# Moving the operands' rows from 128 to 64 bytes past the weights' rows, modulo 256

## The chip, the cores and the metric

The kernel runs on one core of a Trainium2 chip. The metric is the device time of one execution in microseconds; the time before is the median of three runs.

## What is computed

One layer of a hybrid decoder trunk in float32, over 16 meta tokens and 256 sequence tokens with a model width of 2048:

```
h = concat(meta, x)                                       # 272 rows of 2048
proj = rmsnorm(h) @ w_in                                  # one input projection, 13336 columns
o_fox = forgetting_attention(fq, fk, fv, ff)              # 8 heads of 128
o_gla = head_rmsnorm(gated_linear_attention(...)) * silu(gr)   # 4 heads
y = sigmoid(gate_fox) * (o_fox @ w_o_fox) + sigmoid(gate_gla) * (o_gla @ w_o_gla)
h = h + y @ w_out
h = h + square(relu(rmsnorm(h) @ w_ff1)) @ w_ff2          # 2048 -> 8192 -> 2048
out = rmsnorm(h)[16:]
```

## The kernel before

**Two halves for each number.** Each float32 matrix product is made from float32r products. An operand and a weight are each split into a high and a low half (a rounding copy on ScalarE, a subtraction on VectorE), and three of the four products are summed in PSUM. Activations stand in SBUF feature by feature on the partitions; a row of an operand holds, for one block k of 128 features, the 256 tokens' high halves and behind them the 256 low halves, 512 numbers or 2048 bytes.

**The pair.** For each k, `mac2` issues two matmuls: `whi` (128x128 weights) against the 512 numbers of the row (line 143), then `wlo` against the 256 high halves (line 144). `gemm2` runs 16 such pairs into one PSUM bank, 8 pairs for the forgetting attention's output. The operands read in this way are `x` (first norm), `og` and `of` (the two branches), `y` (the mixer's sum), `x2` (second norm) and `a` (the squared relu, anew in each of four groups). Each operand has its 16 or 8 rows in one tile made by `operand`, whose argument `at` leaves so many float32 numbers free ahead of the first row.

**The triple.** Where the meta tokens are wanted too, `gemm_all` runs `mac3`: three matmuls of 272 columns for each k, on `x` alone (lines 148, 150 and 152). Here line 148 reads the low halves, whose first number is 64 bytes further on in the row, modulo 256, than the first number that lines 150 and 152 read. A row of `x` is 576 numbers apart from the next, 2304 bytes, so all its rows stand alike modulo 256.

**The order of the reading.** `steps` rearranges the columns of the moving operand and of its result: four numbers (16 bytes) are read, then 48 bytes are skipped; four passes go over the row in this way, each 16 bytes further on.

```
return ap.rearrange("p (i a e) -> p a i e", a=4, e=4)
```

**The weights** come in as 1 MB chunks in the order that `stream()` lists, in two halves, by DMA on SyncE's queue into `raw`. ScalarE copies each into `whi` (line 120) and VectorE subtracts into `wlo` (line 121). Both are pools of five buffers of 4096 bytes, so all weights start at one place modulo 256; in the built program that is byte 128. The operands' tokens start at byte 0 (modulo 256) in the kernel before, so 128 bytes past the weights.

**Elsewhere.** At the start, seven output tiles are fed at once while the first rows arrive: lines 359 and 361 issue up to four matmuls of 512 columns in a row, and then up to four of 256 columns. At the end, line 921 issues 16 matmuls of 256 columns in a row in the stepped order with `wlo`, for each of four output tiles, and line 937 then reads two straight runs of 128 numbers with weights held in `whi_last`, whose place is chosen by itself.

Of the kernel before, what the change touches and what calls it, by code (L numbers as in the profile page):

```python
# [8 lines left out]
F32R = mybir.dt.float32r  # L9
# [7 lines left out]
P = 128  # L17
D = 2048
KT = D // P
# [4 lines left out]
FOX_H, FOX_D = 8, 128  # L24
# [8 lines left out]
NL = 4  # L33
# [32 lines left out]
def trunk(ctx: ExitStack, tc: tile.TileContext, hT, w_small, w_all, consts, w_alpha2, out):  # L66
# [3 lines left out]
    def nm(s):  # L70
        serial[0] += 1
        return f"{s}_{serial[0]}"

    const = ctx.enter_context(tc.tile_pool(name="const", bufs=1))
    keep = ctx.enter_context(tc.tile_pool(name="keep", bufs=1))
# [49 lines left out]
    def next_weights(keep_hi=None):  # L125
        c = chunk[0]
        chunk[0] += 1
        parts = []
        for i in range(2):
            hi, lo, step = weight_half(c, i, None if keep_hi is None else keep_hi[:, HK * i : HK * (i + 1), :])  # L130
            step(0, HK)
            parts.append((hi, lo))
        return lambda k: (parts[k // HK][0][:, k % HK, :], parts[k // HK][1][:, k % HK, :])
# [20 lines left out]
    def gemm2(w, x, k0=0, nk=KT, pool=None):  # L154

        ps = bank(pool or pg, "ps")
        for k in range(nk):
            hi, lo = w(k0 + k)
            mac2(ps, hi, lo, x[:, k], k == 0, k == nk - 1)
        issued()  # L160
        return ps
# [69 lines left out]
    def operand(pool, name, nk=KT, at=0, **kw):  # L231

        t = pool.tile([P, at + nk * 2 * NT], F32R, name=nm(name), **kw)
        return t[:, at:].rearrange("p (k o t) -> p k o t", o=2, t=NT)
# [2 lines left out]
    h = keep.tile([P, KT, NA + 3], F32, name="h")  # L237

    ROW = 576
    x_row = keep.tile([P, 32 + KT * ROW + 32], F32R, tag="s1", name="x")[:, 32 : 32 + KT * ROW].rearrange(  # L240
        "p (k r) -> p k r", r=ROW)[:, :, 0 : 2 * NA]
    x_hi, x_lo = x_row[:, :, 0:NA], x_row[:, :, NA:]
    x = x_row[:, :, NM : NM + 2 * NT].rearrange("p k (o t) -> p k o t", t=NT)
# [22 lines left out]
    def gain(i, k):  # L266
        return h[:, k, NA + i : NA + i + 1]
# [60 lines left out]
    for s in range(KT // 2):  # L328
# [22 lines left out]
        at = [(w[0][:, c], w[1][:, c]) for w, n in ((wa, 4), (wb, 3)) for c in range(n)]  # L351
# [113 lines left out]
    og_box = []  # L465

    def og_tile():
        if not og_box:
            og_box.append(operand(keep, "og", at=48, tag="s2"))
        return og_box[0]  # L470

    def gla_gates(ts):
# [30 lines left out]
    def gla_head(hd, sg, ready=None):  # L503
# [129 lines left out]
        def scale():  # L633
            for i in range(4):
                j = 4 * hd + i
                nc.vector.scalar_tensor_tensor(oT[:, i, :], oT[:, i, :], ggn[:, j : j + 1], rg, op0=ALU.mult,
                                               op1=ALU.mult)
                nc.vector.tensor_tensor(oT[:, i, :], oT[:, i, :], st["sg"][:, i, :], op=ALU.mult)
                split_to(og_tile()[:, j, 0, :], og_tile()[:, j, 1, :], oT[:, i, :])
# [44 lines left out]
    for hd in range(1, GLA_H):  # L684
        gla_head(hd, None)
    flush()
    og = og_tile()


    cum.close()  # L690
    branches = ExitStack()
    late = branches.enter_context(tc.tile_pool(name="late", bufs=1, reuse_waits="tile"))
    of = operand(late, "of", FOX_H, at=16)
    negc = late.tile([P, FOX_H, NA], F32, name="negc")
    nc.gpsimd.dma_start(negc.rearrange("p h t -> p (h t)"), fdram.to_broadcast([P, FOX_H * NA]))
    fox = ExitStack()
# [137 lines left out]
    for j0 in range(0, KT, 2):  # L834
# [5 lines left out]
        for j in range(2):  # L840
            t = total(gemm2(next_weights(), og))
            nc.vector.tensor_tensor(t, gates[2 * j + 1], t, op=ALU.mult)
            nc.vector.tensor_tensor(yf[:, j0 + j, :], gates[2 * j], t, op=ALU.add)
    y = operand(keep, "y", at=48, tag="s1")
    for j in range(KT):
        split_to(y[:, j, 0, :], y[:, j, 1, :], yf[:, j, :])
    mix.close()
# [3 lines left out]


    ht = h[:, :, NM:NA]
    x2 = operand(keep, "x2", at=48, tag="s2")

    def square_sum(j, acc):
        if j == 0:
            nc.scalar.activation(acc, ht[:, j, :], AF.Square)
        else:
            sq = gat.tile([P, NT], F32, tag="hsq", name=nm("hsq"))  # L860
            nc.scalar.activation(sq, ht[:, j, :], AF.Square)  # L861
            nc.gpsimd.tensor_tensor(acc, acc, sq, op=ALU.add)  # L862

    def add_residual(j, ps):
        b = tmp.tile([P, NT], F32, tag="evb", name=nm("evb"))
        nc.scalar.copy(b, ps[:, NT:512])
        nc.vector.tensor_tensor(ht[:, j, :], ps[:, 0:NT], ht[:, j, :], op=ALU.add)
        nc.vector.tensor_tensor(ht[:, j, :], ht[:, j, :], b, op=ALU.add)
# [16 lines left out]
    def relu2(a, f, ps):  # L885
        t = total(ps)
        nc.vector.scalar_tensor_tensor(t, t, 0.0, r2b, op0=ALU.max, op1=ALU.mult)
        s = gat.tile([P, NT], F32, tag="asq", name=nm("asq"))
        nc.vector.tensor_tensor(s, t, t, op=ALU.mult)
        split_to(a[:, f, 0, :], a[:, f, 1, :], s)  # L890

    acc = gat.tile([P, NT], F32, tag="acc", name="acc3", bufs=1)
    for g in range(NG):
        a = operand(keep, "a", at=48, tag="s1")
        held = []
        for f in range(KT):
            ps = gemm2(next_weights(), x2, pool=px if g == 0 and f < 3 else pg)
            if g == 0 and f == 0:
                held.append(ps)
                continue  # L900
            if g == 0 and f == 1:
                relu2(a, 0, held.pop())
            relu2(a, f, ps)
        last = g == NG - 1
        for j in range(KT - NL if last else KT):
            add_residual(j, gemm2(next_weights(), a))
            if last:
                square_sum(j, acc)
                nc.scalar.activation(ht[:, j, :], ht[:, j, :], AF.Identity, scale=gain(2, j))
                if j == 0:  # L910
                    tc.keep_in_program_order(nc.scalar.preload_act_table_set("natural_log_exp_and_others"))


    whi = keep.tile([P, 0 + NL * KT * P + 64], F32R, tag="s2", name="whi_last")[:, 0 : 0 + NL * KT * P].rearrange(
        "p (n k m) -> p n k m", k=KT, m=P)
    ends = []
    for n in range(NL):
# [150 lines left out]
```

## Time and profile before

| what | value |
|---|---|
| median of three runs (lowest to highest) | 1540.71 us (1538.93 to 1549.66) |
| the profiled execution: its time, its span | 1539.45 us, 1537.7 us |
| mean granted TensorE clock | 0.999 |
| TensorE matmuls: busy, number | 99% of the span, 9812 |
| TensorE weight loads: busy, number | 91%, 9812 |
| VectorE, ScalarE, GpSimd busy | 69%, 51%, 8% |
| share of TensorE in the chain that ended last | 93% |

Matmuls are pipelined: one starts long before the one ahead of it has ended. The duration of a matmul's record therefore says little of its cost. What one costs is the time from its start to the start of the next, and that is read from the view in order of time, or from the number of matmuls in a stretch of known length.

### The profile page before, as it was taken

The page shows a single profiled execution, that of the slowest core. Times are in us where ns is not written, and L with a number is a line of the kernel's source. Part 1 is how long each engine was busy: PE and PEld are TensorE (multiplying, and loading weights), DVE is VectorE, ACT ScalarE, POOL GpSimd, SP SyncE. Part 2 cuts the span into 40 slices and gives each one's busy share as a digit, 9 for nine tenths or more (in the row PEclk, how much of TensorE's full clock was granted, in tenths as well). Part 3 has the DMA queues.
Part 4 walks back from the last instruction along what each step waited for, and adds up shares of the span by engine and source line. Part 5 has one row for each costly group of instructions (what it writes and reads, how often), then busy time and mean ns, then how long its engine had stood idle before and what let it go on. Part 6 is the DMA issues. An engine that isn't in the chain of part 4 may idle for free.

```text
span 1537.7 us, 25427 instructions
## 1 busy us (share of the span) xinstructions
PE 1525.8 (99%) x9812; PEld 1399.2 (91%) x9812; DVE 1059.2 (69%) x1659; ACT 791.0 (51%) x1271; POOL 128.3 (8%) x213
## 2 busy tenths in 40 slices
PE   9999999999999999999999999999999999999997
PEld 8999999999998888899888899889899889888887
DVE  7898858686666655656777876567765776667765
ACT  7766444455555444444565554444544544445563
POOL 5012000011100000000011000000000000000022
PEclk9999999999999999999999999999999999999999
DMA  9544545455555555555565555555565556655552
GB/s 309 180 162 168 179 160 187 161 207 171 166 170 180 199 198 196 201 194 200 183 210 200 191 194 200 196 198 199 192 204 195 199 198 194 200 196 200 193 195 97
DMA packets 86602, 293.09 MB, mean 191 GB/s; under 512 B 9112, under 2 KB 16800, under 8 KB 86352
## 3 DMA queue, kind: packets, MB, share of 16 engines
q1 hardware_dynamic: 85872, 289.62, 55.8%
q8 instruction: 77, 1.26, 0.3%
q0 software_dynamic: 176, 1.12, 0.2%
q10 hardware_dynamic: 432, 0.72, 0.1%
q14 instruction: 45, 0.37, 0.1%
HBM read 289.32 MB, written 2.11 MB: 190 GB/s over the span
## 4 chain that ended last, share of the span: by engine, by line
PE 93%; DVE 2%; DMA 1%; ACT 1%; issue 1%; POOL 1%; SPq 0%; POOLq 0%; ACTq 0%; DVEq 0%
PE ps L143 51%; PE ps L144 26%; PE psa L152 4%; PE psa L148 4%; PE psa L150 4%; DMA raw<-w_all_dram 1%; DVE wlo L121 1%; PE ps L937 1%; PE pa L557 1%; PE ps L921 0%; ACT whi L120 0%; PE po L620 0%; POOL o L985 0%; ACT whi L292 0%; POOL room L340 0%
## 5 line engine op out<-in xcount | busy, mean ns | idle before, releaser
L121 DVE TENSOR_TENSOR wlo<-raw,whi 128x1024 fp32r<-128x1024 f32 x522 | 640.3, 1227 | 399.2 <-ACT whi L120 390.9
L120 ACT CAST whi<-raw 128x1024 fp32r<-128x1024 f32 x522 | 548.9, 1052 | 601.6 <-PE ps L143 532.4
L143 PE MATMUL ps<-x,whi 128*128 128x512 f32 x1952 | 655.7, 383 | 0.8 <-DVE x L874 0.8
L144 PE MATMUL ps<-x,wlo 128*128 128x256 f32 x1952 | 533.3, 273 | 0.0
L143 PEld LDWEIGHTS ps<-x,whi 128*128 128x128 f32 x1952 | 366.4, 188 | 65.5 <-DVE x L874 1.1
L144 PEld LDWEIGHTS ps<-x,wlo 128*128 128x128 f32 x1952 | 366.8, 188 | 0.1
L143 PE MATMUL ps<-a,whi 128*128 128x512 f32 x960 | 319.9, 382 | 0.0
L144 PE MATMUL ps<-a,wlo 128*128 128x256 f32 x960 | 261.4, 273 | 0.0
L143 PEld LDWEIGHTS ps<-a,whi 128*128 128x128 f32 x960 | 179.9, 188 | 31.8
L148 PE MATMUL psa<-x,whi 128*128 128x272 f32 x640 | 183.1, 287 | 0.0
L152 PE MATMUL psa<-x,whi 128*128 128x272 f32 x640 | 181.5, 284 | 0.0
L144 PEld LDWEIGHTS ps<-a,wlo 128*128 128x128 f32 x960 | 180.4, 188 | 0.3
L150 PE MATMUL psa<-x,wlo 128*128 128x272 f32 x624 | 176.8, 283 | 0.0
L148 PEld LDWEIGHTS psa<-x,whi 128*128 128x128 f32 x640 | 120.0, 187 | 0.3
L152 PEld LDWEIGHTS psa<-x,whi 128*128 128x128 f32 x640 | 120.0, 188 | 0.0
L150 PEld LDWEIGHTS psa<-x,wlo 128*128 128x128 f32 x624 | 117.2, 188 | 0.0
L862 POOL TENSOR_TENSOR acc<-acc,hsq 128x256 f32<-128x256 f32 x26 | 28.5, 1094 | 735.5 <-ACT hsq L861 735.5
L143 PE MATMUL ps<-og,whi 128*128 128x512 f32 x256 | 85.9, 382 | 0.0
L143 PE MATMUL ps<-y,whi 128*128 128x512 f32 x256 | 85.3, 382 | 0.0
L144 PE MATMUL ps<-og,wlo 128*128 128x256 f32 x256 | 69.9, 273 | 0.0
L144 PE MATMUL ps<-y,wlo 128*128 128x256 f32 x256 | 69.7, 273 | 0.0
L184 DVE TENSOR_TENSOR evt<-ps,evb 128x256 f32<-128x256 f32 x158 | 65.7, 416 | 0.5 <-ACT evb L181 0.5
(297 smaller groups left out, 1419.6 us busy)
## 6 DMA issues: line engine op xcount, KB each, us to landing
raw<-w_all_dram SPq DMA_DIRECT2D x537, 512.0 KB, 3.6
raw<-w_all_dram SPq DMA_DIRECT2D x8, 384.0 KB, 7.0
h<-hT_dram SPq DMA_DIRECT2D x8, 275.0 KB, 6.7
negc<-fdram POOLq DMA_DIRECT2D x1, 1088.0 KB, 8.2
out_dram<-o SPq DMA_DIRECT2D x2, 512.0 KB, 2.6
raw<-w_all_dram SPq DMA_DIRECT2D x2, 256.0 KB, 4.0
room<-w_small_dram SPq DMA_DIRECT2D x1, 320.0 KB, 7.6
out_dram<-o ACTq DMA_DIRECT2D x1, 320.0 KB, 3.1
```

Source lines behind the costliest of these rows:

```text
L120: nc.scalar.copy(hi[:, k, :], r)
L121: nc.vector.tensor_tensor(lo[:, k, :], r, hi[:, k, :].bitcast(F32), op=ALU.subtract)
L143: nc.tensor.matmul(steps(ps), hi, steps(row(x)), start=first, stop=False)
L144: nc.tensor.matmul(steps(ps[:, 0:NT]), lo, steps(x[:, 0, :]), start=False, stop=last)
L148: nc.tensor.matmul(steps(ps[:, X_LO]), hi, steps(x_lo[:, k]), start=first, stop=False, skip_group_check=True)
L150: nc.tensor.matmul(steps(ps[:, 0:NA]), lo, steps(x_hi[:, k]), start=False, stop=last and hi is None, skip_group_check=True)
L152: nc.tensor.matmul(steps(ps[:, 0:NA]), hi, steps(x_hi[:, k]), start=False, stop=last, skip_group_check=True)
L184: nc.vector.tensor_tensor(t, ps[:, 0:NT], b, op=ALU.add)
L557: nc.tensor.matmul(dst, k[:, a], q[:, a, :], start=(a == 0), stop=(a == 1))
L862: nc.gpsimd.tensor_tensor(acc, acc, sq, op=ALU.add)
L937: nc.tensor.matmul(ps[:, NT:], w(k)[0], a[:, k, :, tok], start=(k == 0), stop=(k == KT - 1))
```

## The change

Each place that sets the first byte of an operand's rows is moved by 64 bytes, 16 numbers: `at` falls by 16 for `of`, `og`, `y`, `x2` and `a`, and the 32 numbers ahead of the first row of `x` become 16. Against the weights the pairs' rows then stand at 64 instead of 128 bytes modulo 256, the low halves in the triple at 64 instead of 128, and the high halves in the triple at 0 instead of 64. `whi_last` is moved by as much, so line 937 reads at the same distance (192) as before. No instruction is added, removed or put elsewhere on any engine.

```diff
-    x_row = keep.tile([P, 32 + KT * ROW + 32], F32R, tag="s1", name="x")[:, 32 : 32 + KT * ROW].rearrange(
+    x_row = keep.tile([P, 16 + KT * ROW + 48], F32R, tag="s1", name="x")[:, 16 : 16 + KT * ROW].rearrange(
...
-            og_box.append(operand(keep, "og", at=48, tag="s2"))
+            og_box.append(operand(keep, "og", at=32, tag="s2"))
...
-    of = operand(late, "of", FOX_H, at=16)
+    of = operand(late, "of", FOX_H, at=0)
...
-    y = operand(keep, "y", at=48, tag="s1")
+    y = operand(keep, "y", at=32, tag="s1")
...
-    x2 = operand(keep, "x2", at=48, tag="s2")
+    x2 = operand(keep, "x2", at=32, tag="s2")
...
-        a = operand(keep, "a", at=48, tag="s1")
+        a = operand(keep, "a", at=32, tag="s1")
...
-    whi = keep.tile([P, 0 + NL * KT * P + 64], F32R, tag="s2", name="whi_last")[:, 0 : 0 + NL * KT * P].rearrange(
+    whi = keep.tile([P, 48 + NL * KT * P + 16], F32R, tag="s2", name="whi_last")[:, 48 : 48 + NL * KT * P].rearrange(
```

## The prediction

> **What bounds the kernel now.** I read first the page's head, for what runs all the time, and its chain of work that ended last, for what sets the end.
>
> ```profile
> span 1537.7 us, 25427 instructions
> PE 1525.8 (99%) x9812; PEld 1399.2 (91%) x9812; DVE 1059.2 (69%) x1659; ACT 791.0 (51%) x1271; POOL 128.3 (8%) x213
> PE 93%; DVE 2%; DMA 1%; ACT 1%; issue 1%; POOL 1%; SPq 0%; POOLq 0%; ACTq 0%; DVEq 0%
> L120 ACT CAST whi<-raw 128x1024 fp32r<-128x1024 f32 x522 | 548.9, 1052 | 601.6 <-PE ps L143 532.4
> ```
>
> TensorE is 93% of the chain, and ScalarE's splitting of the weights, the work that feeds it, stands idle for 532.4 us until TensorE's pairs free a buffer. Weights are always there ahead of time. So the time is set by how fast TensorE gets through its matmuls, and nothing else has to be followed unless TensorE became faster by far more than is at stake here.
>
> Second, the groups by shape, for the number of pairs, and the busy time by stretch, for what a pair costs.
>
> ```profile
> L143 PE MATMUL ps<-x,whi 128*128 128x512 f32 x1952 | 655.7, 383 | 0.8 <-DVE x L874 0.8
> L143 PE MATMUL ps<-a,whi 128*128 128x512 f32 x960 | 319.9, 382 | 0.0
> L143 PE MATMUL ps<-og,whi 128*128 128x512 f32 x256 | 85.9, 382 | 0.0
> L143 PE MATMUL ps<-y,whi 128*128 128x512 f32 x256 | 85.3, 382 | 0.0
> L143 PE MATMUL ps<-of,whi 128*128 128x512 f32 x128 | 43.2, 383 | 0.0
> ...
> 900.00:1000.00 100.00, 100.00 (x603) 89.99 (x602) 65.07 (x90) 46.93 (x63) 0.00 (x0) 1.00 0.58 196
> 1000.00:1200.00 200.00, 200.00 (x1203) 179.98 (x1202) 134.06 (x186) 94.52 (x131) 0.00 (x0) 1.00 0.59 198
> 1200.00:1500.00 300.00, 300.00 (x1803) 269.95 (x1802) 203.81 (x286) 153.64 (x222) 11.36 (x9) 1.00 0.59 197
> ```
>
> There are 1952 + 960 + 256 + 256 + 128 = 3552 pairs (`x` in these names takes in `x2`). In the stretches, which hold pairs alone, 100, 200 and 300 us hold 603, 1203 and 1803 matmuls: past three that reach over the edges it is 600 for each 100 us, 300 pairs, 333.3 ns for one, at a granted clock of 1.00. The pairs take 3552 x 333.3 ns = 1184 us, 77% of the span.
>
> Third, the instructions in order of time, for how a pair is made up. Columns: start, duration, instruction; the two last rows are the weight loads of the same time.
>
> ```profile
> 799.65 0.38 PE L143 MATMUL ps<-y,whi 128*128 128x512 f32 x1
> 799.87 0.27 PE L144 MATMUL ps<-y,wlo 128*128 128x256 f32 x1
> 799.98 0.38 PE L143 MATMUL ps<-y,whi 128*128 128x512 f32 x1
> ...
> 805.98 0.38 PE L143 MATMUL ps<-y,whi 128*128 128x512 f32 x1
> ...
> 799.87 0.19 PEld L143 LDWEIGHTS ps<-y,whi 128*128 128x128 f32 x1
> 799.99 0.19 PEld L144 LDWEIGHTS ps<-y,wlo 128*128 128x128 f32 x1
> ```
>
> From 799.65 to 805.98 there are 19 pairs, 333.2 ns each. From start to start the 512-column matmul takes 0.22 us (0.2216 over the 19) and the 256-column one 0.11 (0.1116). Each next load of weights starts with a matmul: that for line 143 at 799.87, with line 144, and that for line 144 at 799.99, with line 143. So TensorE reads two things from SBUF side by side, the row that streams and the weights that come next, and the change sets how these two addresses stand to each other. That is the only thing it does.
>
> **What the trace says of two readings side by side.** The same shapes, in the same stepped order and at the same 128 bytes, do not always cost the same:
>
> ```profile
> 30.39 1.05 PE L359 MATMUL ps<-x,whi 128*128 128x512 f32 x4
> 31.28 0.63 PE L361 MATMUL ps<-x,wlo 128*128 128x256 f32 x4
> 31.75 1.07 PE L359 MATMUL ps<-x,whi 128*128 128x512 f32 x4
> 32.66 0.62 PE L361 MATMUL ps<-x,wlo 128*128 128x256 f32 x4
> 33.13 0.61 PE L359 MATMUL ps<-x,whi 128*128 128x512 f32 x2
> ...
> 1505.80 5.50 PE ps L921 x48
> 1514.97 7.28 PE ps L937 x64
> ```
>
> In the prologue four 512-column matmuls take 0.89 and 0.91 us (30.39 to 31.28, 31.75 to 32.66), 222.5 and 227.5 ns each, against 221.6 in the pair. Four of 256 columns take 0.47 us twice, 117.5 ns each, and the 48 of line 921 take 5.50 us, 114.6 ns each, against 111.6. What differs is only the moment in the stream at which a load falls: in the pair it repeats exactly, elsewhere it wanders. I read this as the two readings now and then meeting in one part of SBUF, with one of them waiting a nanosecond or two; that they meet is inferred, no row names it. The pair would then be locked in a favourable position, and 64 bytes shift that position.
>
> **The change part by part.**
>
> *Removed, added, moved between engines:* nothing; all five queues issue the same rows in the same order. Other tiles behind `of` slide by 64 bytes, which touches some hundred matmuls of the attention heads: at 3 ns each that is 0.3 us, taken as nothing. Where ScalarE and VectorE write the operands is off the path (51% and 69% busy); the longest such step would have to last longer than the weights' lead to count.
>
> *The pairs, 128 to 64 bytes.* No row of before has pairs at 64. From above, the position out of lock bounds it: 225.0 ns (mean of 222.5 and 227.5) for 512 columns and 116.0 (mean of 114.6 and 117.5) for 256, together 341.0, 7.7 ns more than 333.3. From below: nothing excludes a better position. The two gaps differ by 110.0 ns for 256 columns, so 768 columns stream in 330 ns; the rows are rounded to 10 ns, and by the average's error of a nanosecond or so this may as well be 327. A pair can lose 3 to 6 ns, no more. Between the ends I take +5.6 ns. The 256-column matmul has the load of the next weights beside its whole length, so it takes the full price out of lock, 116.0 - 111.6 = 4.4, of which I keep 3.5 for the nanosecond of error in 111.6. The 512-column one has a load beside about half of its columns (the next one follows 0.11 to 0.12 us after a load's start where it waits for it), so it takes half of 225.0 - 221.6 = 3.4, some 1.7, and 0.4 for the same error. That is 3552 x 5.6 ns = +19.9 us.
>
> *The triple.* Here before has both distances side by side.
>
> ```profile
> 202.94 0.28 PE L150 MATMUL psa<-x,wlo 128*128 128x272 f32 x1
> 203.06 0.28 PE L152 MATMUL psa<-x,whi 128*128 128x272 f32 x1
> 203.18 0.28 PE L148 MATMUL psa<-x,whi 128*128 128x272 f32 x1
> 203.30 0.28 PE L150 MATMUL psa<-x,wlo 128*128 128x272 f32 x1
> ...
> 205.39 0.28 PE L148 MATMUL psa<-x,whi 128*128 128x272 f32 x1
> ...
> L148 PE MATMUL psa<-x,whi 128*128 128x272 f32 x640 | 183.1, 287 | 0.0
> ```
>
> Line 148 reads at 128 and lines 150 and 152 at 64, and each takes 0.12 us. From 203.18 to 205.39 six triples take 2.21 us, 122.8 ns per matmul. So line 148, moved to 64, should cost what it did. Lines 150 and 152 go to 0, for which no row in stepped order exists; in 1280 matmuls, by the spread of the 256-column rows (114.6 to 117.5, 3 ns) that is 4 us either way, taken as 0.
>
> *The prologue and the end.* Lines 359, 361 and 921 are out of lock already, some 260 matmuls, by 3 ns under 1 us. Line 937 keeps its 192 bytes: 113.8 ns (7.28 us for 64) stays.
>
> *Sum:* 1537.7 + 19.9 = 1557.6 us of span; with the 1.8 us around the span of the profiled execution (1539.45 - 1537.7) it is 1559.4. The median of the runs lies 1.3 us above that execution, so on its scale 1560.6; I say 1560.
>
> **The rule that speaks against it.** The Trainium skill, "TensorE: Matmul & The Clock Gate", section "Step-by-step: what each phase is for", gives TensorE two independent ports into SBUF and says: "Loading the next tile's weights doesn't steal SBUF read bandwidth from the running matmul." By that rule the distance between row and weights cannot matter, and the time stays at 1540.7. The trace does not refute it outright, since the triple's rows are alike at 128 and 64, but it leaves no reason why 256 columns should take 111.6 ns in the pair and 114.6 to 117.5 elsewhere. This is the first rival.
>
> **The rivals.**
>
> *Nothing changes* (the readings don't meet, or 64 is as good as 128 for the pair too). For it: the triple, 122.8 ns at both distances. Against it: the spread of equal instructions above, and that a triple of 272 columns wanders anyway, so it would not show a lock. It gives 1540.7, with 5 us either way for lines 150 and 152.
>
> *Faster:* 64 bytes put the pair in a better position and it sheds the larger part of its 3 to 6 ns, 4.3 on average. That is 3552 x 4.3 = 15.3 us less, 1525. The place is the gap between lines 144 and 143 in every pair. It decides once the pair falls below 329 ns. For it speaks that 333.3 is above 327 to 330; against it, that no run of equal matmuls in the trace, in whatever position, costs less per column than the pair does.
>
> *Out of lock entirely:* both matmuls cost what they do in the prologue, 7.7 ns more, and lines 150 and 152 pay 3 ns each. That is 27.4 + 3.8 = 31 us, 1572; with the dearest rows (227.5 + 117.5 = 345.0) 41.6 + 3.8 = 45 us, 1586. For it: a new distance has no reason to be locked at all. Against it: the pair's pattern repeats exactly, so that it will be locked somewhere.
>
> **How the numbers follow.** About 1% (15 us) is what a measurement of this kernel can tell from no change. Slower by the sum or more, both slower cases together: 0.52, of which the partly lost lock at 1560 has 0.37 and the full loss 0.15. Nothing changes: 0.36. Faster: 0.12. The slower case begins at 1556.1; where the lock costs under 4.3 ns a pair it falls inside 1%, which takes 0.06 from slower to same; of the faster case a fifth, 0.02, falls inside too. So faster 0.10, same 0.44, slower 0.46. The likeliest case's own range is 1549 (only the 256-column matmul pays, 2.3 ns) to 1572. The range that should hold 8 in 10 reaches over "nothing" and half way into "faster", 1530, and up to 1582, a little short of the dearest rows.
>
> **What would show each step.** In the busy time by stretch, 200 us of pairs alone between 1000 and 1200 should hold some 1180 matmuls in place of 1203 (338.9 ns a pair). In order of time the gap from line 144 to line 143 should go from 0.11 to about 0.115, that from 143 to 144 from 0.22 to about 0.224. The triples should stay at 0.12 a matmul. Line 921's group of 48 should stay within 5.4 to 5.7 us, and line 937's 64 at 7.28. VectorE's and ScalarE's busy time must not move, and ScalarE's idle time before line 120 should rise by about what TensorE loses. The prediction is wrong if a pair takes 333 ns still (the rule above, or a lock that doesn't depend on the 64 bytes), if it falls below 333, or if the time moves while the pairs don't, which would put the cause into the triples' distance of 0.

## The result

| | kernel before | kernel after |
|---|---|---|
| median of 20 runs | 1548.24 us | 1539.10 us |
| lowest to highest | 1538.29 to 1549.66 | 1537.84 to 1540.75 |
| profiled execution: time, span | 1539.45, 1537.7 | 1538.62, 1536.8 |

After over before is 0.9967, with a 95% interval of 0.9951 to 0.9982: faster by a third of a per cent, where slower by 1.3% was forecast. The kernel before has no middle: 9 of its 20 runs lie near 1539 us and 11 near 1548.5 us, with nothing between. All 20 of the changed kernel lie near 1539. Both groups of the kernel before are in the ratio, which compares means; its median only says which group has more runs. What the change gave is that the dearer group is gone; against the cheaper one it gained nothing that the runs tell apart.

The profile of before that the prediction read is of the cheaper group. Against it, the page's head and chain of after show the same balance. TensorE's share of the chain is now 97% instead of 93%; that is not the change's doing, since a copy of the kernel before (`e4_again`, below) shows 96%:

```profile
span 1536.8 us, 25427 instructions
PE 1525.6 (99%) x9812; PEld 1402.4 (91%) x9812; DVE 1059.5 (69%) x1659; ACT 789.6 (51%) x1271; POOL 127.6 (8%) x213
PE 97%; DVE 1%; ACT 1%; issue 0%; POOL 0%; DMA 0%; POOLq 0%; ACTq 0%; DVEq 0%
```

The busy time by stretch (from:to, length, busy time of TensorE and number of matmuls, then the other engines) answers to the rows of before:

```profile
100.00:460.00 360.00, 360.00 (x2655) 344.74 (x2654) 259.12 (x497) 185.28 (x353) 39.01 (x87) 1.00 0.53 174
1000.00:1200.00 200.00, 200.00 (x1202) 180.60 (x1201) 134.03 (x187) 94.38 (x130) 0.00 (x0) 1.00 0.60 198
1200.00:1500.00 300.00, 300.00 (x1802) 270.90 (x1801) 203.36 (x287) 153.01 (x220) 11.68 (x9) 1.00 0.61 197
```

Again 600 matmuls in 100 us (1802 - 1202): a pair takes 333.3 ns at 64 bytes as at 128. In order of time:

```profile
799.58 0.38 PE L143 MATMUL ps<-y,whi 128*128 128x512 f32 x1
799.80 0.27 PE L144 MATMUL ps<-y,wlo 128*128 128x256 f32 x1
799.92 0.38 PE L143 MATMUL ps<-y,whi 128*128 128x512 f32 x1
...
806.92 0.38 PE L143 MATMUL ps<-y,whi 128*128 128x512 f32 x1
...
1504.86 5.58 PE ps L921 x48
1514.12 7.25 PE ps L937 x64
```

22 pairs in 7.34 us are 333.6 ns each, within the rounding of the rows. Lines 921 and 937 take 5.58 and 7.25 us where before had 5.50 and 7.28. The pair's period has not moved. What has moved a little is its division: averaged over the pairs between 1020 and 1100 us, the 512-column matmul takes 220.0 ns to the next start where before it took 221.3, and the 256-column one 113.3 instead of 112.1.

### The profile page after: what moved, and what is told of

It is laid out like the page before. It is cut to its first block, busy times and chain, and to the rows that moved or that the text cites. A ratio compares the mean times of both kernels' runs of the same rounds, so it can differ in the third digit from the quotient of the medians.

```text
span 1536.8 us, 25427 instructions
## 1 busy us (share of the span) xinstructions
PE 1525.6 (99%) x9812; PEld 1402.4 (91%) x9812; DVE 1059.5 (69%) x1659; ACT 789.6 (51%) x1271; POOL 127.6 (8%) x213
## 4 chain that ended last, share of the span: by engine, by line
PE 97%; DVE 1%; ACT 1%; issue 0%; POOL 0%; DMA 0%; POOLq 0%; ACTq 0%; DVEq 0%
PE ps L143 51%; PE ps L144 26%; PE psa L152 5%; PE psa L148 5%; PE psa L150 4%; PE ps L359 1%; PE ps L361 1%; PE ps L937 1%; PE pa L557 1%; PE ps L921 0%; DVE wlo L121 0%; ACT whi L120 0%; PE po L620 0%; DMA h<-hT_dram 0%; POOL o L985 0%
## 5 line engine op out<-in xcount | busy, mean ns | idle before, releaser
L120 ACT CAST whi<-raw 128x1024 fp32r<-128x1024 f32 x522 | 546.9, 1048 | 604.7 <-PE ps L143 534.0
```

Of the source, the lines that this page charges most:

```text
L120: nc.scalar.copy(hi[:, k, :], r)
```

## The experiments

All kernels below issue what the kernel before issues, in its order on every engine, except `e3_straight` (another column order) and `e9_regular` (one spot of the order in each group of the MLP). Beside each of them the kernel before ran on the same chip. Where a pair's time is read from a count, it is 400 us over the number of matmuls between 1000 and 1200 us less three at the edges; a count is good to about one matmul, 0.3 ns, and it is an average where the period changes on the way. A period "from start to start" is the mean over a long unbroken row of pairs in the trace, and good to about 0.1 ns.

**Does the distance matter at all?** Theory 1: the row that streams and the weights being loaded get in each other's way, depending on their distance. Theory 2: they don't, and all distances cost alike. Three kernels tell them apart. `e1_zero` and `e2_192` only change the first byte, for instance

```diff
-    x2 = operand(keep, "x2", at=48, tag="s2")
+    x2 = operand(keep, "x2", at=16, tag="s2")     # e1_zero: 0 bytes from the weights
+    x2 = operand(keep, "x2", at=64, tag="s2")     # e2_192: 192 bytes
```

and all other operands with it. `e3_straight` leaves the bytes where they are and reads straight on:

```diff
-        return ap.rearrange("p (i a e) -> p a i e", a=4, e=4)
+        return ap
```

> All pairs read at 0 bytes from the weights (modulo 256), line 148 at 0, lines 150 and 152 at 192; line 937 stays at 192. Theory 1 (readings meet; 128 and 64 are both good positions, others need not be): the pair of 512 and 256 columns goes from 333.3 to 335 to 341 ns, 3552 pairs, so 6 to 27 us more, 1545 to 1566 us. Theory 2 (distances in steps of 64 bytes are all one to the pair): 333.3 ns and 1539 us, within 3 us.

> All pairs read at 192 bytes from the weights, line 148 at 192, lines 150 and 152 at 128; line 937 stays at 192. Theory 1: another price again, 333 to 341 ns a pair, 1539 to 1566 us; theory 2: 333.3 ns and 1539 us, within 3 us.

> Distances as before (128), but the columns are read straight on in place of the stepped order, in all pairs and triples. Theory 1: weights and row, read in the same order, meet at each crossing; 256 columns read straight take 118 to 120 ns in the attention heads of the kernel before, so the pair takes 338 to 345 ns, 17 to 42 us more, 1556 to 1581 us. Theory 2 (the pair's period is its columns and a fixed cost): 333.3 ns and 1539 us.

Measured: 1564.23 us at 0 bytes (ratio 1.0142, 1.0098 to 1.0186), 1550.52 us at 192 (1.0044, 1.0021 to 1.0066), 1605.38 us straight on (1.0411, 1.0373 to 1.0448). The busy time by stretch, in this order:

```profile
1000.00:1200.00 200.00, 200.00 (x1179) 176.62 (x1178) 129.65 (x180) 92.55 (x127) 0.00 (x0) 1.00 0.61 194
...
1000.00:1200.00 200.00, 200.00 (x1190) 177.58 (x1189) 131.22 (x181) 93.15 (x129) 0.00 (x0) 1.00 0.61 195
...
1000.00:1200.00 200.00, 200.00 (x1142) 175.31 (x1141) 126.77 (x176) 88.85 (x122) 0.00 (x0) 1.00 0.59 188
```

A pair takes 340.1, 337.0 and 351.2 ns at a granted clock of 1.00. Times 3552 pairs that is 24, 13 and 64 us over 333.3 ns; the kernels are 25, 11 and 66 us over 1539. Theory 2 is out: the same instructions on other addresses cost up to 1.6% more, and the stepped order is worth 66 us. (`e3_straight` changes the order of the result in PSUM along with that of the row, since `steps` is applied to both; which of the two costs the time was not separated.) Straight reading came out beyond the range set for it (338 to 345 ns a pair).

**What is the dearer group of the kernel before?** First a copy of it, for a profile that might fall there.

> The kernel before, unchanged. Its runs so far fall into two groups, near 1539 and near 1548.4 us, those of the changed kernel only near 1539. Theory 1: the dearer group is a second position of the pairs, so a profile that falls into it shows the pair at about 336 ns (9.4 us over 3552 pairs is 2.6 ns each). Theory 3: the dearer group lies outside the pairs (start, transfers, end), and the pair is at 333.3 ns in both.

Ten runs, two near 1539 and eight near 1548.5; the profiled one was at 1539.32 and told nothing. Then parts of the change, and the kernel before once more:

```diff
-    x2 = operand(keep, "x2", at=48, tag="s2")      # e5_ff: x2, a and whi_last as in the change, the rest as before
+    x2 = operand(keep, "x2", at=32, tag="s2")
-    x_row = keep.tile([P, 32 + KT * ROW + 32], ...)[:, 32 : 32 + KT * ROW]     # e6_x: x alone as in the change
+    x_row = keep.tile([P, 16 + KT * ROW + 48], ...)[:, 16 : 16 + KT * ROW]
```

> Only x2 and a (1984 of the 3552 pairs, and line 921) move to 64 bytes; x, og, of and y stay at 128. Theory 1 (the dearer group of the kernel before, 9.3 us, is a second position of all pairs at 128, 2.6 ns each): 1568 pairs keep it, so two groups 4.1 us apart, near 1539 and 1543. Theory 3 (it lies outside the pairs): the dearer group stays at 1548, or is gone altogether if the moved tiles alone hold it.

> Only x moves to 64 bytes (928 pairs, the prologue, and the triples to 64 and 0); the other 2624 pairs stay at 128. Theory 1: two groups 6.9 us apart, near 1539 and 1546. Theory 3: 9.3 us apart, or one group only if the triples or the prologue hold it.

> The kernel before once more, for a profile of its dearer group (more than half of its runs so far). If it falls there: theory 1 about 336 ns a pair over all pairs, theory 3 333.3 ns and the time elsewhere. If it falls near 1539 us it tells nothing.

`e5_ff`: four runs between 1539.0 and 1540.2, one group (ratio 0.9960, 0.9924 to 0.9995). `e6_x`: 1543.9, 1544.0, 1544.9 and 1553.7, still two groups 9 us apart, with 5 us on top. `e8_look` fell at 1549.03 us, into the dearer group. So theory 1, as it was put for these runs (all pairs 2.6 ns dearer), is wrong, and so is theory 3, that it lies outside the pairs. With `x2` and `a` alone moved the group did not appear. Four runs are few (with 49 of 86 runs dear, four cheap ones in a row come up by chance once in 29), but the profile of `e8_look` shows that the group does live in the MLP, and how. Busy time by stretch, first before (cheaper group), then `e8_look`, the same program:

```profile
850.00:930.00 80.00, 80.00 (x483) 72.01 (x482) 62.85 (x102) 40.28 (x61) 0.00 (x0) 1.00 0.58 195
1020.00:1100.00 80.00, 80.00 (x483) 71.99 (x482) 59.27 (x91) 40.43 (x60) 0.00 (x0) 1.00 0.59 198
1190.00:1270.00 80.00, 80.00 (x483) 71.97 (x482) 59.26 (x90) 40.43 (x60) 0.00 (x0) 1.00 0.58 197
1360.00:1440.00 80.00, 80.00 (x483) 71.98 (x482) 59.27 (x89) 40.10 (x60) 0.00 (x0) 1.00 0.58 198
```

```profile
850.00:930.00 80.00, 80.00 (x482) 71.97 (x481) 62.85 (x102) 40.25 (x61) 0.00 (x0) 1.00 0.61 195
1020.00:1100.00 80.00, 80.00 (x470) 70.70 (x469) 57.18 (x86) 39.05 (x58) 0.00 (x0) 1.00 0.58 192
1190.00:1270.00 80.00, 80.00 (x482) 72.01 (x481) 58.53 (x88) 40.11 (x59) 0.00 (x0) 1.00 0.61 198
1360.00:1440.00 80.00, 80.00 (x470) 70.70 (x469) 56.83 (x86) 38.30 (x57) 0.00 (x0) 1.00 0.59 191
```

In the second and fourth stretch 467 matmuls (470 less three at the edges) fit where before has 480: 342.6 ns a pair by this count, at the same clock. In the others it is 333.3 as before. The stream changes over at single places. In order of time (a count x2 is two matmuls of one line in a row), first the kernel before and the changed kernel at this place, then `e8_look` at the first change and at the change back:

```profile
937.98 0.60 PE L143 MATMUL ps<-a,whi 128*128 128x512 f32 x2
...
936.98 0.60 PE L143 MATMUL ps<-a,whi 128*128 128x512 f32 x2
...
938.11 0.60 PE L143 MATMUL ps<-a,whi 128*128 128x512 f32 x2
938.55 0.40 PE L144 MATMUL ps<-a,wlo 128*128 128x256 f32 x2
938.79 0.39 PE L143 MATMUL ps<-a,whi 128*128 128x512 f32 x1
...
941.19 0.39 PE L143 MATMUL ps<-a,whi 128*128 128x512 f32 x1
...
1113.33 0.61 PE L143 MATMUL ps<-a,whi 128*128 128x512 f32 x2
1113.79 0.39 PE L144 MATMUL ps<-a,wlo 128*128 128x256 f32 x2
```

From 938.79 to 941.19 seven pairs take 2.40 us, 342.9 ns each; from start to start over the whole stretch it is 342.2. Both places are the same spot of the program: early in the second MLP product the scheduler has put the last pair of the first tile, which waits for the last row of `a`, into the middle of a pair of the next tile, so that two matmuls of 512 columns follow each other and then two of 256. From 938 to 1113, and again from the spot in the third group to that in the fourth, some 350 us go at 342.2 instead of 333.3 ns: 350 x (1 - 333.3 / 342.2) = 9.1 us, nearly all of the 9.5 us between the groups. In the two profiles of the cheaper group (before, `e4_again`) the odd spots are there too, and the period stays.

Is that spot the trigger, or only where it shows? `e9_regular` keeps all distances at 128 and lets the odd pair come between two whole pairs (`mac2` now returns its second matmul for this):

```diff
+    def two_first(x):
+        w0, ps0 = next_weights(), bank(pg, "ps")
+        for k in range(KT - 1):
+            mac2(ps0, *w0(k), x[:, k], k == 0, False)
+        w1, ps1 = next_weights(), bank(pg, "ps")
+        for k in range(12):
+            mm = mac2(ps1, *w1(k), x[:, k], k == 0, False)
+        with tc.issue_after(mm.ins):
+            mm = mac2(ps0, *w0(KT - 1), x[:, KT - 1], False, True)
+        with tc.issue_after(mm.ins):
+            for k in range(12, KT):
+                mac2(ps1, *w1(k), x[:, k], False, k == KT - 1)
...
+        done = two_first(a)
...
-            add_residual(j, gemm2(next_weights(), a))
+            add_residual(j, done[j] if j < 2 else gemm2(next_weights(), a))
```

> The kernel before, all distances 128, but at the start of each second MLP product the last pair of its first tile stands between two whole pairs of the next tile, where the scheduler had put it between line 143 and line 144 of one pair (two of 512 columns, then two of 256). Theory 4 (that irregular spot is where the stream falls from the 333.3 ns position into the 342 ns one, in some executions): all runs near 1539 us, no group near 1548. Theory 5 (the fall has another cause, for instance transfers or the tile's start, and only shows there): two groups as before, about half of the runs near 1548.

Twelve runs, all between 1538.4 and 1539.7 us, median 1539.31; beside them the kernel before had 8 of 16 near 1548.5 (ratio 0.9965, 0.9945 to 0.9985). In the view in order of time the pairs run through the place one by one:

```profile
937.96 0.38 PE L143 MATMUL ps<-a,whi 128*128 128x512 f32 x1
938.18 0.27 PE L144 MATMUL ps<-a,wlo 128*128 128x256 f32 x1
938.29 0.38 PE L143 MATMUL ps<-a,whi 128*128 128x512 f32 x1
```

Theory 4 holds: without the odd spot the dearer group is gone, at 128 bytes, by the same 0.35% that the change gave. Over the whole study 49 of 86 runs of the kernel before were in the dearer group, none of the 12 of this kernel and none of the 20 of the changed one. A fifth spot of this kind, at 763.8 us in the mixer's output product, is left in `e9_regular`; neither in its profile nor in that of `e8_look` does the period change there.

`e6_x` shows the same from another side. Its 5 us come from two places. The first row below is the start of four tiles of `x`, which stands at 64 bytes there, the second the start of `of` behind them; the third and fourth are the ends of a stretch of `og`, which stayed at 128; the fifth is the odd spot in `y`, also at 128:

```profile
495.21 0.39 PE L143 MATMUL ps<-x,whi 128*128 128x512 f32 x1
...
516.97 0.39 PE L143 MATMUL ps<-of,whi 128*128 128x512 f32 x1
...
522.33 0.38 PE L143 MATMUL ps<-og,whi 128*128 128x512 f32 x1
...
533.00 0.39 PE L143 MATMUL ps<-x,whi 128*128 128x512 f32 x1
...
765.88 0.60 PE L143 MATMUL ps<-y,whi 128*128 128x512 f32 x2
```

The 64 pairs of `x` take 21.76 us, 340.0 ns each, at the same 64 bytes at which the changed kernel's `x` runs at 333.3 in the same place; the 32 pairs of `og` take 10.67 us, 333.4 each. There are seven such stretches of `x` up to 744 us, with `of` and `og` between them: 448 x 6.7 ns = 3.0 us. The pairs of `y` run at 333.3 ns up to the odd spot at 765.88 us and at 342.2 behind it, for some 79 us more: 2.1 us. So one distance has more than one price, and in this one profile a stream comes into the dearer one at an odd spot or by alternating with rows at another distance.

**Is 333.3 ns the floor, and how do the distances go?** All operands were moved to 96, 80, 112, 32, 48, 160 and 224 bytes, each by the same kind of edit as `e1_zero`; for instance

```diff
-    y = operand(keep, "y", at=48, tag="s1")
+    y = operand(keep, "y", at=40, tag="s1")       # e7_96
+    y = operand(keep, "y", at=36, tag="s1")       # e10_80
```

> All rows at 96 bytes from the weights, half way between the two kernels (line 148 at 96, lines 150 and 152 at 32; line 937 stays at 192). Theory 1: the price depends on where load and row meet in steps under 64 bytes, and 96 lies between two good positions or on a dearer one: 333 to 341 ns a pair, 1538 to 1566 us. Theory 2b (only the distance in steps of 64 bytes counts, and 64 and 128 are both good): 333.3 ns, 1539 us.

> All rows at 80 bytes from the weights (line 148 at 80, lines 150 and 152 at 16; line 937 stays). Theory 1 (each distance has its own few positions, in steps of 16 bytes; 64, 96 and 128 share one at 333.3 ns): 333 to 342 ns a pair, 1538 to 1570 us. Theory 6 (333.3 ns is the floor of a pair however it is placed): never under 333.3 ns, so never under 1536 us.

> All rows at 112 bytes from the weights (line 148 at 112, lines 150 and 152 at 48; line 937 stays). Theory 1: 333 to 342 ns a pair, 1538 to 1570 us. Theory 6: never under 333.3 ns, so never under 1536 us.

> All rows at 32 bytes from the weights (line 148 at 32, lines 150 and 152 at 224; line 937 stays). Theory 1: between 0 (340 and 344 ns) and 64 (333.3 ns), so 333 to 344 ns a pair, 1538 to 1575 us. Theory 6: never under 333.3 ns, so never under 1536 us.

> All rows at 48 bytes from the weights (line 148 at 48, lines 150 and 152 at 240; line 937 stays). Theory 6 (333.3 ns is the least a pair can take): 333.3 ns or more, 1538 us or more; by its neighbours 32 (340 ns) and 64 (333.3), and as 80 and 112 are dear, 336 to 345 ns, 1548 to 1580 us. Theory 7 (64 and 128 are alike by coincidence): some distance is cheaper, under 333 ns and under 1537 us.

> All rows at 160 bytes from the weights (line 148 at 160, lines 150 and 152 at 96; line 937 stays). Theory 6: 333.3 ns or more; between 128 (333.3) and 192 (336.7), as 96 is between 64 and 128, 333 to 337 ns, 1538 to 1552 us. Theory 7: under 333 ns and under 1537 us possible.

> All rows at 224 bytes from the weights (line 148 at 224, lines 150 and 152 at 160; line 937 stays). Theory 6: 333.3 ns or more; between 192 (336.7) and 0 (340), 336 to 341 ns, 1548 to 1566 us. Theory 7: under 333 ns possible.

| bytes from the weights | matmuls from 1000 to 1200 us | a pair by this count, ns | periods from start to start, from 500 us on, ns | median, us | ratio to before (interval) |
|---|---|---|---|---|---|
| 0 | 1179 | 340.1 | 340.0; 343.3 in the MLP up to its first odd spot | 1564.2 | 1.0142 (1.0098 to 1.0186) |
| 32 | 1178 | 340.4 | 340.0 | 1561.1 | 1.0099 (1.0067 to 1.0131) |
| 48 | 1202 | 333.6 | 333.3; 340.0 in the MLP up to its first odd spot | 1542.2 | 0.9991 (0.9969 to 1.0013) |
| 64 (after) | 1202 | 333.6 | 333.3 | 1539.1 | 0.9967 (0.9951 to 0.9982) |
| 80 | 1165 | 344.2 | 342.7 and 346.7 in turn | 1576.0 | 1.0196 (1.0158 to 1.0234) |
| 96 | 1201 | 333.9 | 333.3; 336.7 in the MLP up to its first odd spot | 1542.5 | 0.9981 (0.9945 to 1.0018) |
| 112 | 1178 | 340.4 | 340.0 | 1563.2 | 1.0114 (1.0082 to 1.0147) |
| 128 (before) | 1203 | 333.3, or 342.6 in parts | 333.3, or 342.2 in parts | 1539 or 1548.5 | |
| 160 | 1181 | 339.6 | 339.2 | 1559.6 | 1.0113 (1.0068 to 1.0158) |
| 192 | 1190 | 337.0 | 336.7 | 1550.5 | 1.0044 (1.0021 to 1.0066) |
| 224 | 1169 | 343.1 | 342.7 | 1572.0 | 1.0193 (1.0155 to 1.0231) |

The ratios compare with all runs of the kernel before on the same chip, and its share of dear runs differed (8 of 16 in one set, 5 of 13 in another). Against its cheaper group, 48 and 96 bytes cost some 3 us, though their ratios lie below 1. The results at 80, 160 and 224 bytes came out above the ranges set for them and that at 48 below; the other distances fell inside.

The rows on which the dearest and the two cheapest new distances rest: for 80 bytes the stretch of the table, one on each side of the odd spot, and that spot; for 48 the stretch of the table; for 96 two stretches on either side of the odd spot:

```profile
1000.00:1200.00 200.00, 200.00 (x1165) 176.60 (x1164) 128.94 (x177) 90.71 (x125) 0.00 (x0) 1.00 0.60 192
960.00:1130.00 170.00, 170.00 (x995) 150.42 (x994) 111.34 (x156) 77.03 (x107) 0.00 (x0) 1.00 0.61 195
1135.00:1305.00 170.00, 170.00 (x982) 149.48 (x982) 111.09 (x156) 77.18 (x108) 0.00 (x0) 1.00 0.60 193
...
1131.35 0.62 PE L143 MATMUL ps<-a,whi 128*128 128x512 f32 x2
...
1000.00:1200.00 200.00, 200.00 (x1202) 179.84 (x1201) 132.75 (x184) 94.27 (x130) 0.00 (x0) 1.00 0.60 198
...
860.00:930.00 70.00, 70.00 (x418) 62.72 (x418) 54.36 (x88) 35.29 (x55) 0.00 (x0) 1.00 0.60 196
960.00:1030.00 70.00, 70.00 (x422) 63.01 (x420) 43.14 (x55) 31.07 (x40) 0.00 (x0) 1.00 0.62 199
```

No distance of eleven goes below 333.3 ns, so theory 6 stands as far as it was tried and theory 7 has nothing for it. The price does not follow steps of 64 bytes (theory 2b): 16 bytes from 64 to 80 cost 37 us. Nor is it a smooth curve between neighbours, as the expectations for 48 and 160 assumed. The odd spots of the MLP are where the period changes in these kernels too, with all addresses unchanged. At 80 bytes it goes from 342.7 to 346.7 ns at 1131.35 us, back at the next group's spot (1308.84) and up again at the last one (1484.29). At 96, 48 and 0 bytes it falls at the first group's spot (940.05, 940.38 and 951.43 us) from 336.7, 340.0 and 343.3 to 333.3, 333.3 and 340.0 ns. No version beats the changed kernel; `e9_regular` at 128 bytes is as good.

## Why the prediction was wrong, step by step

*What bounds the kernel* was right: over the cheaper group of the kernel before, the kernels' times rise by the pair's time by count, less 333.3 ns, times 3552, within some 3 us at every distance and for the straight order.

*"I read this as the two readings now and then meeting"*, one of them waiting: that the place of the row matters is shown by the eleven distances. That the row meets the load of the weights is still inferred. For it speaks that the row's address alone cannot set the price, since at an odd spot, where only the order of the 512- and 256-column matmuls is disturbed, the period changes with all addresses as they were. But only the rows were ever moved, never the weights, and no run leaves the loads out. What the prediction drew from the Trainium skill's rule against it ("TensorE: Matmul & The Clock Gate", section "Step-by-step: what each phase is for"), that the distance cannot matter, is refuted here: with instructions, order and clock unchanged, the time went from 1539 to 1576 us by addresses alone. Whether the rule itself is at fault is not shown.

*The pairs, 128 to 64 bytes, "+5.6 ns": this is the term that failed.* It measured 0.0 (333.3 ns from start to start at both distances), so 19.9 us of loss did not come. Its parts were +3.5 ns for the 256-column matmul and +2.1 for the 512-column one; the runs showed +1.2 and -1.3, which cancel. The term priced a new distance by the mean of rows in which the same distance is passed at changing moments (lines 359, 361 and 921). But a pair repeats, and a repeating stream settles into an exact period; the wandering mean of similar rows says nothing on which. Dearer periods than 333.3 do exist, by 3.4 to 13.4 ns, at 0, 32, 80, 112, 160, 192 and 224 bytes, in parts at 48, 96 and 128, and at 64 itself when `x` alone stands there (340.0). Why the changed kernel at 64 holds 333.3 stays open, and none of the rows that the prediction shows tells it. That the lock at 128 was "a favourable position" was right, since no lower period was found; that it can be lost within one execution was not foreseen.

*The rival "nothing changes"* has the nearest time, 1540.7, and of its two reasons the second fits, "64 is as good as 128 for the pair too"; the first, that the readings don't meet, leaves the eleven distances without a reason. The measured 1539.1 lies inside the stated range, 1530 to 1582, because that range was drawn to take in this rival. Triples and the pairs among them kept their pace: from 100 to 460 us 2655 matmuls against 2654. A triple by itself, from start to start, took 365.5 ns instead of 368.2, over 640 of them 1.7 us, within the 4 us either way kept for lines 150 and 152 at 0 bytes.

*The base.* The prediction's sum rested on one profile at 1539.45 us and passed over a sign in the times it was given: of three runs one stood at 1549.66. That run was of the dearer group, and the only measurable effect of the change lay there.

*Lines 921 and 937, VectorE and ScalarE* stayed as forecast (5.58 and 7.25 us; 1059.5 and 789.6 us busy). ScalarE's longer wait before line 120 did not come (534.0 against 532.4 us for TensorE), since TensorE lost nothing.

## What to carry to other kernels

On a kernel that TensorE bounds, the place of the moving rows, and the order of their columns, belong to the tuning: here 4% between the stepped and the straight order and 2.4% between 64 and 80 bytes, with no instruction added or removed. Measure it distance by distance, since neither neighbours nor means of similar instructions predict it, and with all operands moved, since `x` alone at 64 bytes cost 5 us where all of them at 64 cost nothing. And where runs of one kernel fall into two groups, profile until both are seen and compare them by stretch: an odd spot in the order can decide which of two positions hundreds of pairs keep.

## What had not been expected of the hardware

The pair's period takes exact values and holds each for tens of microseconds, in the kernels above 333.3, 336.7, 339.2, 340.0, 342.2, 342.7, 343.3, 346.7 and 351.1 ns. The same program, at the same clock and addresses, can hold 333.3 or 342.2 ns over 175 us and change at one spot, where the alternation of 512- and 256-column matmuls is disturbed. The grain of the addresses is fine: from 64 to 80 bytes a pair goes from 333.3 to 342.7 or 346.7 ns. The Trainium skill ("SBUF — State Buffer", section "Specifications (TRN2)") gives SBUF lines of 16 bytes; the jump within 16 bytes agrees with a grain no coarser than that, though smaller shifts were not tried.

Open remain: what tips one execution at 128 bytes and not another; why the odd spot, which the changed kernel has too, never threw it out of 333.3 ns in 20 runs; whether the distance to the weights counts, by which all places are given here, or the row's place against something else, since the weights were not moved; which of the two readings waits. The dearer group of the kernel before and `e6_x` were each profiled once. From `e6_x`, the stretch of `y` that holds its odd spot, with 342.2 ns behind it:

```profile
760.00:840.00 80.00, 80.00 (x470) 70.81 (x469) 58.75 (x75) 45.27 (x73) 11.64 (x12) 1.00 0.61 199
```
